# A decoder trunk on one core: the weight sums of a seven-product FFN step made in place, splits and sums in a fixed order, plain half steps between

## The chip, the cores and the metric

One core of a Trainium2 chip runs the whole kernel. The metric is device time in microseconds (us). TensorE (PE in the profile) multiplies, VectorE (DVE) and ScalarE (ACT) work element by element, SyncE (SP) issues the loads.

## What is computed

A two-layer decoder trunk in float32, 256 tokens of width 2048. Each layer has a mixer and a dense FFN, and it is the FFN that the change touches:

```python
D_MODEL = 2048; SEQ = 256; DEPTH = 2
D_FF = ((8 * D_MODEL + 3 * 256 - 1) // (3 * 256)) * 256     # 5632

def swiglu_ffn(h, w_gate, w_up, w_down):
    return (jax.nn.silu(h @ w_gate) * (h @ w_up)) @ w_down

for i in range(DEPTH):
    ...                                                     # mixer, residual
    f = swiglu_ffn(rms_norm(h, norm_gains[i, 2]), ffn_w_gate[i], ffn_w_up[i], ffn_w_down[i])
    h = h + rms_norm(f, norm_gains[i, 3])
```

## The kernel before

**Three matmuls for one.** Every float32 product is made of rounded parts. ACT copies a tile to a rounded high part (`whi`), DVE subtracts it from the tile to get the low part (`wlo`), and `mm3` (L212 to L214) issues three matmuls: high times high, high times low, low times high. So each weight that is loaded costs one ACT copy and one DVE subtraction: a split. There are four `whi` and four `wlo` buffers. They are handed out in the order of the splits, so a split takes the buffers of the one four before it and waits until TensorE has read those.

**The FFN.** Gate and up columns stand interleaved in blocks of 256. The 5632 hidden columns are made in five stages of 2, 2, 2, 2 and 3 chunks of 1024 gate-and-up columns; after each stage the down projection (`to_tokens`) uses what the stage made. The first stage is plain. In the other four, each chunk is 512 columns by plain products (`plain_step`) and 512 by a scheme of seven products in place of eight 2x2 block products (`seven_step`), four steps of each, over groups `g` of the 2048 rows. The seven-product step needs sums of weight blocks; DVE makes them in a room of its own (`ws`, tag `gb`, two buffers): three additions of 1024, 512 and 512 elements a partition. After the fourth step `seven_hidden` puts the seven products together, applies silu and multiplies; `hidden` does so for the plain half. `to_features` then turns the result on TensorE by four transposes (L418) and splits it again (L166, L167).

**PSUM.** Eight banks in two sets of four. `g4()` hands out the sets in turn. A stage takes one set for the seven products (`seven`) and the other for the plain half and the transposes (`other`). The next `g4()`, that of the down projection, is the set of `seven` again. In the order listings below, in one such stage, `seven` is bank2_78, bank3_79, bank6_82 and bank7_83; `other` is bank0_76, bank1_77 and, for transposes, bank4_80 and bank5_81.

**Order.** A scheduler sorts the instructions of each engine when the program is built; on the chip each engine then runs its list in that order, and an instruction that waits holds up all behind it on its engine. `issue_after` (here `behind`) puts one instruction behind another. The order of a chunk before:

```python
seven_step(col, g, seven)
if g == 3:
    behind_done()
    seven_hidden(seven, c * 4)
plain_step(col + 512, g, other[:2])
...
hidden(other[:2], c * 4 + 2, False)
```

Weights come through a ring of three tiles of 2048 elements a partition (`wst`). SP issues all loads in order.

Of the kernel before, what the change touches and what calls it, by code (L numbers as in the profile page):

```python
# [17 lines left out]
P = 128  # L18
# [30 lines left out]
def trunk(ctx, tc, x, mem, positions, norm_gains, w_mem_kv, w_down, a_w_in, a_b_s, a_w_out, w_kv_a, w_uk, w_uv,  # L49
# [118 lines left out]
        return ins.ins  # L168

    def wtile():  # L170
        return wpool.tile([P, 2048], F32, tag="wst", name="wst", bufs=3)

    def wsplit(src, n, gain=None):

# [101 lines left out]
                          in1=R.rearrange("p (o t) -> p o t", o=1).broadcast_to([P, n, S]), op=ALU.mult)  # L276

    def gain_bcast(i, j):
        g = tmp.tile([P, D], F32, tag="gb", name="gb", bufs=2)
        sp.dma_start(out=g, in_=norm_gains[i, j:j + 1, :].broadcast_to([P, D]))  # L280
        return g

# [119 lines left out]
    def ffn(i, xp, r, R, gcol, each, hp, need):  # L402
# [39 lines left out]
        def normalise(g):  # L442


            room = tmp.tile([P, D], F32, tag="gb", name="xr", bufs=2)
# [23 lines left out]
        def stage(col, g):  # L469

            st = wtile().rearrange("p (h k n) -> p h k n", h=2, k=2)
            rows = w_gate_up[i].rearrange("(h k p) n -> p h k n", h=2, p=P)
            for e in range(2):
                sp.dma_start(out=st[:, e], in_=rows[:, e, 2 * g:2 * g + 2, col:col + 512])
            return st

        def parts_of_sum(src, n=1024):
            hi = wpool.tile([P, 1024], F32R, tag="whi", name="whi", bufs=4)
            lo = wpool.tile([P, 1024], F32R, tag="wlo", name="wlo", bufs=4)
            hv, lv = hi[:, :n], lo[:, :n]  # L480
            if len(src.shape) == 4:
                hv, lv = [t.rearrange("p (h k n) -> p h k n", h=2, k=2) for t in (hv, lv)]
            elif len(src.shape) == 3:
                hv, lv = [t.rearrange("p (k n) -> p k n", k=2) for t in (hv, lv)]
            split(hv, lv, src)
            return hi, lo

        def seven_step(col, g, X):
            st = stage(col, g)
            room = tmp.tile([P, D], F32, tag="gb", name="ws", bufs=2)  # L490
            t13, t24 = room[:, :1024], room[:, 1024:]
            b11, b21, b22 = st[:, 0, :, :S], st[:, 1, :, :S], st[:, 1, :, S:]
            sums = room.rearrange("p (s k n) -> p s k n", s=4, k=2)
# [9 lines left out]
            wt = parts_of_sum(st[:, :, :, :S])  # L503
            dve.tensor_tensor(out=sums[:, 0:2], in0=st[:, :, :, S:], in1=st[:, 0].rearrange("p k (x n) -> p x k n", x=2),  # L504
                              op=ALU.add)
            products(wt, (xp, 0, 0, X[0][:, :S], True), (xp, 8, 0, X[0][:, S:], False))
            wt = parts_of_sum(t13)
            dve.tensor_tensor(out=sums[:, 2], in0=sums[:, 1], in1=b11, op=ALU.add)
            products(wt, (sz, 0, 0, X[1][:, S:], True), (sx, 0, 0, X[1][:, :S], False))
            dve.tensor_tensor(out=sums[:, 3], in0=sums[:, 2], in1=b21, op=ALU.add)  # L510
            wt = parts_of_sum(t24)
            products(wt, (sz, 0, 1, X[3][:, :S], True), (xp, 8, 1, X[2][:, :S], True))
            wt = parts_of_sum(b22, 512)
            products(wt, (sx, 0, 1, X[2][:, S:], False))

        def seven_hidden(X, f):

            m1, m2, m5, m6 = X[0][:, :S], X[0][:, S:], X[1][:, S:], X[3][:, :S]
            v = tmp.tile([P, 512], F32, tag="lat", name="v", bufs=2)
            act.copy(out=v[:, :S], in_=m1)  # L520
            dve.tensor_tensor(out=v[:, S:], in0=m6, in1=v[:, :S], op=ALU.add)
            u = tmp.tile([P, 512], F32, tag="lat", name="u", bufs=2)
            dve.tensor_tensor(out=u.rearrange("p (x n) -> p x n", x=2), in0=X[1].rearrange("p (x n) -> p x n", x=2),
                              in1=v[:, S:].rearrange("p (o n) -> p o n", o=1).broadcast_to([P, 2, S]), op=ALU.add)
            dve.tensor_tensor(out=m1, in0=m2, in1=v[:, :S], op=ALU.add)
            sg = tmp.tile([P, 512], F32, tag="sg", name="sg")
            act.activation(out=sg[:, :S], in_=m1, func=AF.Silu)
            dve.tensor_tensor(out=X[2], in0=X[2], in1=u, op=ALU.add)
            act.activation(out=sg[:, S:], in_=X[2][:, :S], func=AF.Silu)
            dve.tensor_tensor(out=m5, in0=m5, in1=u[:, :S], op=ALU.add)  # L530
            hv = tmp.tile([P, 512], F32, tag="hv", name="hv")
            for b, o in enumerate((X[2][:, S:], m5)):
# [5 lines left out]
        def plain_step(col, g, banks):  # L538
            st = stage(col, g)
            for e in range(2):  # L540
                wt = wsplit(st[:, e].rearrange("p k n -> p (k n)"), 1024)
# [17 lines left out]
        for pi, (c0, ncn) in enumerate(parts):  # L559
            if pi == 0:  # L560
# [30 lines left out]

            def gate(k):
# [31 lines left out]
    def start():  # L624
# [7 lines left out]
        m = []  # L632
        for b in range(2):
            yield
            t = tmp.tile([P, D], F32, tag="gb", name="memt", bufs=2)
            sp.dma_start(out=t, in_=mem[0, b * P:(b + 1) * P, :])
            m.append(t)
        yield
        yield from norm_scale(m, r_m, R_m)

# [77 lines left out]

    with tc.tile_pool(name="mixa", bufs=1) as ma:

        wT = tmp.tile([P, NH, P], F32, tag="gb", name="wT", bufs=2)
# [410 lines left out]
```

## Time and profile before

| | |
|---|---|
| median of 3 runs | 2118.49 us (2117.72 to 2119.36) |
| profiled execution: time, span in the trace | 2121.68 us, 2120.0 us |
| PE, DVE, ACT busy | 99%, 74%, 53% of the span |
| granted TensorE clock, mean | 0.998 |
| DMA engines busy | 56.4% by the kernel's queue |

The span runs from the first to the last instruction of the trace; the profiled execution takes 1.68 us more. TensorE's matmuls are pipelined and the ends that the profile gives are modelled, so that "busy" hides short pauses: the distance between the starts of two matmuls tells more than their length.

### The profile page before, as it was taken

What the parts mean: (1) busy time and instruction counts of PE and PEld (TensorE: products, weight loads), DVE (VectorE), ACT (ScalarE), POOL (GpSimd) and SP (SyncE); (2) the same over time, 40 slices, a digit from 0 to 9 for tenths busy, and PEclk for the clock granted to TensorE, in tenths of its full rate; (3) what the DMA queues carried; (4) which work ended last, traced back from release to release, by engine and by line L of the source; (5) the groups of instructions that cost most, each with busy time, mean ns of one, the idle gap of its engine ahead of it and who ended that gap; (6) DMA issues with size and microseconds to landing.
All of it is one profiled execution on the core that took longest, in us unless ns stands there. A gap on an engine that the chain in (4) does not pass through costs nothing.

```text
span 2120.0 us, 30041 instructions
## 1 busy us (share of the span) xinstructions
PE 2094.3 (99%) x11922; PEld 1835.1 (87%) x11922; DVE 1568.0 (74%) x2151; ACT 1119.4 (53%) x1478; POOL 4.1 (0%) x11
## 2 busy tenths in 40 slices
PE   8999999999999999999999999999999999999998
PEld 7889989788888888889889998978888888889987
DVE  6556755976868878689767775597686877868966
ACT  6544444655545545455545654565554554545543
POOL 0000000000000000000000000000000000000000
PEclk9999999999999999999999999999999999999999
DMA  9655365555565655655754534555556565565563
GB/s 359 250 181 174 92 221 185 178 181 177 195 202 179 201 179 186 209 178 199 242 176 136 181 122 140 183 174 189 177 190 200 178 218 179 189 207 168 199 222 130
DMA packets 153981, 398.96 MB, mean 188 GB/s; under 512 B 9456, under 2 KB 16880, under 8 KB 152816
## 3 DMA queue, kind: packets, MB, share of 16 engines
q1 hardware_dynamic: 153840, 397.05, 56.4%
q8 instruction: 93, 1.52, 0.3%
q14 instruction: 48, 0.39, 0.1%
HBM read 394.91 MB, written 2.10 MB: 187 GB/s over the span
## 4 chain that ended last, share of the span: by engine, by line
PE 91%; DVE 5%; DMA 2%; ACT 1%; issue 1%; SPq 0%; DVEq 0%; ACTq 0%
PE bank L214 29%; PE bank L213 29%; PE bank L212 29%; DMA wst<-in_w_gate_up 2%; PE bank L418 1%; DVE wlo L181 1%; DVE wlo L187 1%; DVE h L362 1%; PE bank L240 0%; PE bank L1016 0%; PE bank L1017 0%; DVE ws L504 0%; PE bank L707 0%; PE bank L1041 0%; DVE wlo L167 0%
## 5 line engine op out<-in xcount | busy, mean ns | idle before, releaser
L212 PE MATMUL bank<-whi,hl 128*128 128x512 f32 (+3 forms) x2880 | 1030.8, 359 | 0.9 <-ACT hl L166 0.7
L213 PE MATMUL bank<-wlo,hl 128*128 128x512 f32 (+3 forms) x2880 | 1026.6, 356 | 3.6 <-DVE wlo L181 1.9
L214 PE MATMUL bank<-whi,hl 128*128 128x512 f32 (+3 forms) x2880 | 1025.5, 356 | 0.0
L181 DVE TENSOR_TENSOR wlo<-wst,whi 128x1024 fp32r<-128x1024 f32 (+1 forms) x398 | 468.8, 1183 | 237.5 <-ACT whi L179 236.2
L213 PEld LDWEIGHTS bank<-wlo,hl 128*128 128x128 f32 x2880 | 542.3, 188 | 82.1 <-DVE wlo L181 4.1
L214 PEld LDWEIGHTS bank<-whi,hl 128*128 128x128 f32 x2880 | 542.3, 188 | 77.6 <-DVE hl L167 0.5
L212 PEld LDWEIGHTS bank<-whi,hl 128*128 128x128 f32 x2880 | 542.5, 188 | 76.2 <-ACT hl L166 1.9
L179 ACT CAST whi<-wst 128x1024 fp32r<-128x1024 f32 (+1 forms) x398 | 405.0, 1020 | 381.2 <-PE bank L214 346.3
L187 DVE SCALAR_TENSOR_TENSOR wlo<-wst,gains,whi 128x1024 fp32r<-128x1024 f32 (+3 forms) x216 | 255.7, 1193 | 131.0 <-ACT whi L185 128.1
L185 ACT ACTIVATE whi<-wst,gains 128x1024 fp32r<-128x1024 f32 (+3 forms) x216 | 232.2, 1080 | 216.7 <-PE bank L214 131.2
L166 ACT CAST whi<-ws 128x1024 fp32r<-128x1024 f32 x144 | 151.1, 1049 | 159.0 <-PE bank L214 81.0
L167 DVE TENSOR_TENSOR wlo<-ws,whi 128x1024 fp32r<-128x1024 f32 x144 | 175.6, 1220 | 57.0 <-ACT whi L166 56.8
L166 ACT CAST whi<-wst 128x1024 fp32r<-128x1024 f32 (+1 forms) x144 | 120.3, 835 | 108.1 <-PE bank L214 107.3
L167 DVE TENSOR_TENSOR wlo<-wst,whi 128x1024 fp32r<-128x1024 f32 (+1 forms) x144 | 137.0, 951 | 22.0 <-ACT whi L166 22.0
L212 PE MATMUL bank<-hl,whi 128*128 128x256 f32 x448 | 129.1, 288 | 7.0 <-ACT whi L185 7.0
L214 PE MATMUL bank<-hl,wlo 128*128 128x256 f32 x448 | 127.1, 285 | 1.0 <-DVE wlo L187 1.0
L213 PE MATMUL bank<-hl,whi 128*128 128x256 f32 x448 | 127.1, 284 | 0.0
L504 DVE TENSOR_TENSOR ws<-wst 128x1024 f32<-128x1024 f32 x72 | 88.0, 1223 | 26.1 <-DMA wst<-in_w_gate_up 25.7
L212 PEld LDWEIGHTS bank<-hl,whi 128*128 128x128 f32 x448 | 85.2, 190 | 10.2 <-ACT whi L185 7.0
L213 PEld LDWEIGHTS bank<-hl,whi 128*128 128x128 f32 x448 | 85.2, 190 | 2.8
L214 PEld LDWEIGHTS bank<-hl,wlo 128*128 128x128 f32 x448 | 84.8, 190 | 1.5 <-DVE wlo L187 1.4
L213 PE MATMUL bank<-wlo,sx 128*128 128x256 f32 x288 | 81.2, 282 | 0.0
(206 smaller groups left out, 1549.7 us busy)
## 6 DMA issues: line engine op xcount, KB each, us to landing
wst<-in_w_gate_up SPq DMA_DIRECT2D x288, 512.0 KB, 4.5
wst<-in_ffn_w_down SPq DMA_DIRECT2D x76, 1024.0 KB, 5.1
wst<-in_w_gate_up SPq DMA_DIRECT2D x32, 1024.0 KB, 4.9
wst<-in_a_w_in SPq DMA_DIRECT2D x24, 1024.0 KB, 5.1
wst<-in_w_mem_kv SPq DMA_DIRECT2D x15, 1024.0 KB, 6.5
wst<-in_ffn_w_down SPq DMA_DIRECT2D x12, 768.0 KB, 4.5
wst<-in_a_w_out SPq DMA_DIRECT2D x8, 1024.0 KB, 6.0
wst<-in_b_w_in SPq DMA_DIRECT2D x8, 1024.0 KB, 4.9
```

The lines of the kernel that those rows point to most:

```text
L166: ins = act.copy(out=hi, in_=src)
L167: dve.tensor_tensor(out=lo, in0=src, in1=hi.bitcast(F32), op=ALU.subtract)
L179: act.copy(out=hi[:, :n], in_=src)
L181: dve.tensor_tensor(out=lo[:, :n], in0=src, in1=hi[:, :n].bitcast(F32), op=ALU.subtract)
L185: act.activation(out=hi[:, :n], in_=src, func=AF.Copy, scale=g)
L187: dve.scalar_tensor_tensor(out=lo[:, :n], in0=src, scalar=g, in1=hi[:, :n].bitcast(F32), op0=ALU.mult, op1=ALU.subtract)
L212: pe.matmul(out=o, lhsT=a[0], rhs=b[0], start=start, stop=False, **kw)
L213: pe.matmul(out=o, lhsT=a[0], rhs=b[1], start=False, stop=False, **kw)
L214: line["pe"] = pe.matmul(out=o, lhsT=a[1], rhs=b[0], start=False, stop=stop, **kw).ins
L362: ins = dve.scalar_tensor_tensor(out=h[:, b, cs], in0=yv, scalar=rs[b], in1=h[:, b, cs], op0=ALU.mult, op1=ALU.add)
L418: pe.transpose(out=pt[:, q, b, :], in_=hv[:, b * S + q * P:b * S + (q + 1) * P], identity=ident)
L504: dve.tensor_tensor(out=sums[:, 0:2], in0=st[:, :, :, S:], in1=st[:, 0].rearrange("p k (x n) -> p x k n", x=2), op=ALU.add)
```

## The change

The ring of weight tiles has four tiles instead of three, and the rooms of tag `gb` one buffer instead of two (`mem` is read into the tile `h` for its norm). The seven-product step loads its four blocks by four transfers of 256 KB (runs of 1 KB) instead of two of 512 KB (runs of 2 KB), as up, up, gate, gate; first splits what it needs unsummed, then makes the sums in the tile itself, over blocks already split. All splits and sums of these stages are chained in one order. A plain step is cut in halves: one half ahead of the seven-product step, the other between its third product and the remaining four. With this the seven-product half of a chunk comes last, and `seven_hidden` after everything else; it now copies out of PSUM into `u` and `v` instead of summing in the banks. The counts and sizes of matmuls, splits and sums stay as they are.

```diff
-        return wpool.tile([P, 2048], F32, tag="wst", name="wst", bufs=3)
+        return wpool.tile([P, 2048], F32, tag="wst", name="wst", bufs=4)
...
+        def add(out, in0, in1):
+            with behind(last_on["dve"]):
+                after("dve", dve.tensor_tensor(out=out, in0=in0, in1=in1, op=ALU.add))
+
+        def own_split(src):
...
+            with behind(last_on["act"]):
+                after("act", act.copy(out=hi[:, :n], in_=src))
+            with behind(last_on["dve"]):
+                after("dve", dve.tensor_tensor(out=lo[:, :n], in0=src, in1=hi[:, :n].bitcast(F32), op=ALU.subtract))
...
+            for to, e, c in ((2, 0, gate), (3, 1, gate), (0, 1, up), (1, 0, up)):
+                sp.dma_start(out=q[:, to], in_=own[:, e, :, c])
...
+            ups, gates = st[:, :1024], st[:, 1024:]
+            wt = own_split(gates)
             products(wt, (xp, 0, 0, X[0][:, :S], True), (xp, 8, 0, X[0][:, S:], False))
+            wt = own_split(ups[:, :512])
+            products(wt, (sx, 0, 1, X[2][:, S:], True))
+            add(ups, ups, st[:, 512:1536])
+            add(q[:, 2], q[:, 0], q[:, 2])
+            add(q[:, 3], q[:, 2], q[:, 3])
+            between()
+            wt = own_split(ups)
+            products(wt, (sx, 0, 0, X[1][:, :S], True), (sz, 0, 0, X[1][:, S:], False))
+            wt = own_split(gates)
+            products(wt, (sz, 0, 1, X[3][:, :S], True), (xp, 8, 1, X[2][:, :S], False))
...
+            act.copy(out=v[:, :S], in_=X[0][:, :S])
+            dve.tensor_tensor(out=v[:, S:], in0=X[3][:, :S], in1=v[:, :S], op=ALU.add)
+            dve.tensor_tensor(out=v[:, :S], in0=X[0][:, S:], in1=v[:, :S], op=ALU.add)
...
-                        seven_step(col, g, seven)
-                        if g == 3:
-                            behind_done()
-                            seven_hidden(seven, c * 4)
-                        plain_step(col + 512, g, other[:2])
+                        plain = plain_steps(col, g, other[:2])
+                        next(plain)
+
+                        def between():
+                            next(plain)
+                            if g == 3:
+                                behind_done()
+                                hidden(other[:2], c * 4, False)
+
+                        seven_step(col + 512, g, seven, between)
                     behind_done()
-                    hidden(other[:2], c * 4 + 2, False)
+                    seven_hidden(seven, c * 4 + 2)
```

**The seam between a stage and its down projection, on DVE.** Such seams are eight: four stages in each layer. Before, from the first split of the down weights on (L181; `whi` names the split):

```order
L181 TENSOR_TENSOR wlo_5335<-wst_5332,whi_5334 128x1024 [waits DMAHW0_49,Activation_49]
L528 TENSOR_TENSOR bank6_82<-bank6_82,u_5274 128x512 [waits DVE_49,PE_49]
L530 TENSOR_TENSOR bank3_79<-bank3_79,u_5274 128x256
L181 TENSOR_TENSOR wlo_5357<-wst_5332,whi_5356 128x1024 [waits Activation_49]
L534 SCALAR_TENSOR_TENSOR hv_5282<-bank6_82,sg_5277 128x256 [waits Activation_49]
L534 SCALAR_TENSOR_TENSOR hv_5282<-bank3_79,sg_5277 128x256 [waits DVE_49]
L434 TENSOR_TENSOR hv_5327<-bank0_76,sg_5326 128x256 [waits Activation_49]
```

Now, from the same split on (L434 is `hidden`; L530, L531, L533, L535, L536 are the additions of `seven_hidden`):

```order
L181 TENSOR_TENSOR wlo_5341<-wst_5338,whi_5340 128x1024 [waits DMAHW1_49,Activation_49]
L434 TENSOR_TENSOR hv_5281<-bank0_76,sg_5280 128x256 [waits Activation_49]
L434 TENSOR_TENSOR hv_5281<-bank1_77,sg_5280 128x256 [waits Activation_49]
L181 TENSOR_TENSOR wlo_5363<-wst_5338,whi_5362 128x1024 [waits Activation_49]
L181 TENSOR_TENSOR wlo_5381<-wst_5378,whi_5380 128x1024 [waits DMAHW2_49,Activation_49]
L167 TENSOR_TENSOR hl01_73<-bank4_80,hl00_72 128x512 [waits Activation_49]
L530 TENSOR_TENSOR v_5324<-bank7_83,v_5324 128x256 [waits PE_49]
L181 TENSOR_TENSOR wlo_5397<-wst_5378,whi_5396 128x1024 [waits Activation_49]
L531 TENSOR_TENSOR v_5324<-bank2_78,v_5324 128x256 [waits DVE_49]
L533 TENSOR_TENSOR u_5325<-bank3_79,v_5324 128x512
L535 TENSOR_TENSOR v_5324<-bank3_79,u_5325 128x256 [waits DVE_49]
L536 TENSOR_TENSOR u_5325<-bank6_82,u_5325 128x512 [waits DVE_49,PE_49]
```

The plain half's `hv` moved ahead of the seven-product sums, and these now follow the third split of the down weights.

**The same seam on TensorE.** Before, the first matmuls of the down projection, which write bank2_78 first:

```order
L418 MATMUL bank4_80<-ident_84,hv_5282 128x128 x2
L212 MATMUL bank2_78<-whi_5334,hl00_72 128x512 [waits Activation_49]
L213 MATMUL bank2_78<-wlo_5335,hl00_72 128x512
L214 MATMUL bank2_78<-whi_5334,hl01_73 128x512
L212 MATMUL bank3_79<-whi_5334,hl00_72 128x512
```

Now, from the last matmul of the stage on:

```order
L214 MATMUL bank6_82<-whi_5308,hl11_75 128x256
L212 MATMUL bank7_83<-whi_5340,hl00_72 128x512 [waits DVE_49,Activation_49]
L213 MATMUL bank7_83<-wlo_5341,hl00_72 128x512
L214 MATMUL bank7_83<-whi_5340,hl01_73 128x512
L212 MATMUL bank7_83<-whi_5362,hl00_72 128x512 [waits Activation_49]
L213 MATMUL bank7_83<-wlo_5363,hl00_72 128x512
L214 MATMUL bank7_83<-whi_5362,hl01_73 128x512
L212 MATMUL bank7_83<-whi_5380,hl00_72 128x512 [waits Activation_49]
L212 MATMUL bank2_78<-whi_5340,hl00_72 128x512 [waits DVE_49]
```

The down projection now begins with seven matmuls into bank7_83, the first of which waits for DVE.

**From one chunk to the next inside a stage, on DVE.** There are ten such places. Before, from the first addition of `seven_hidden` (L525) on:

```order
L525 TENSOR_TENSOR bank2_78<-bank2_78,v_4839 128x256 [waits Activation_49]
L510 TENSOR_TENSOR ws_4903<-ws_4903,wst_4900 128x512 [waits DVE_49]
L181 TENSOR_TENSOR wlo_4857<-wst_4853,whi_4856 128x1024 [waits DMAHW6_49,Activation_49]
L521 TENSOR_TENSOR v_4839<-bank7_83,v_4839 128x256 [waits PE_49]
L181 TENSOR_TENSOR wlo_4879<-wst_4853,whi_4878 128x1024 [waits DMAHW7_49,Activation_49]
```

Now, from the next chunk's first gate split on (L480 are the sums in the tile; the last row is the split of that chunk's second plain half):

```order
L490 TENSOR_TENSOR wlo_4933<-wst_4927,whi_4932 128x1024 [waits DMAHW4_49,DMAHW3_49,Activation_49]
L490 TENSOR_TENSOR wlo_4949<-wst_4927,whi_4948 128x512 [waits DMAHW5_49,Activation_49]
L167 TENSOR_TENSOR hl01_73<-bank4_80,hl00_72 128x512 [waits Activation_49]
L530 TENSOR_TENSOR v_4888<-bank7_83,v_4888 128x256 [waits PE_49]
L480 TENSOR_TENSOR wst_4927<-wst_4927 128x1024 [waits DMAHW6_49,DVE_49]
L531 TENSOR_TENSOR v_4888<-bank2_78,v_4888 128x256 [waits DVE_49]
L533 TENSOR_TENSOR u_4889<-bank3_79,v_4888 128x512
L480 TENSOR_TENSOR wst_4927<-wst_4927 128x512 [waits DVE_49]
L535 TENSOR_TENSOR v_4888<-bank3_79,u_4889 128x256 [waits DVE_49]
L480 TENSOR_TENSOR wst_4927<-wst_4927 128x512 [waits DVE_49]
L536 TENSOR_TENSOR u_4889<-bank6_82,u_4889 128x512 [waits DVE_49,PE_49]
L490 TENSOR_TENSOR wlo_4962<-wst_4902,whi_4961 128x1024 [waits DMAHW2_49,Activation_49]
```

The additions of `seven_hidden` now stand between the next chunk's weight sums; before, they stood between the splits of the plain step of the same group. On TensorE, where before the whole next seven-product step followed, the list now goes on like this after the first products into bank2_78 (whi_4961 is the second plain half, whi_4977 the summed ups, whi_4948 the single up block):

```order
L214 MATMUL bank2_78<-whi_4932,hl11_75 128x256
L212 MATMUL bank0_76<-whi_4961,hl10_74 128x512 [waits Activation_49]
L212 MATMUL bank1_77<-whi_4961,hl10_74 128x512
L212 MATMUL bank3_79<-whi_4977,sx0_3360 128x256 [waits DVE_49,Activation_49]
L212 MATMUL bank6_82<-whi_4948,sx0_3360 128x256 [waits DVE_49]
L213 MATMUL bank6_82<-wlo_4949,sx0_3360 128x256
```

Three single matmuls were moved ahead of the six into bank6_82, which wait for DVE.

## Rows read from the trace of the kernel before

**Rows 1.** The page: busy us, share of the span, instructions.

```profile
PE 2094.3 (99%) x11922; PEld 1835.1 (87%) x11922; DVE 1568.0 (74%) x2151; ACT 1119.4 (53%) x1478; POOL 4.1 (0%) x11
```

**Rows 2.** Waits of TensorE's weight loads, 512 to 1100 us: total, times, longest.

```profile
PEld bank L213 <- DVE wlo L181: 2.4, 4, 1.6
PEld bank L418 <- DVE hv L534: 1.5, 3, 0.6
```

**Rows 3.** The same waits, 1528 to 2110 us.

```profile
PEld bank L418 <- DVE hv L534: 1.4, 3, 0.6
PEld bank L213 <- DVE wlo L181: 0.8, 2, 0.4
```

**Rows 4.** Timeline, PE at 776 us: start, length, line; twelve and six matmuls.

```profile
775.85 0.40 PE L214 MATMUL bank<-whi,hl 128*128 128x512 f32 x1
...
776.78 0.28 PE L212 MATMUL bank<-whi,hl 128*128 128x256 f32 x1
...
777.38 0.28 PE L214 MATMUL bank<-whi,hl 128*128 128x256 f32 x1
```

**Rows 5.** Timeline, PE at 866 us: the four transposes.

```profile
866.01 0.60 PE L418 MATMUL bank<-ident,hv 128*128 128x128 f32 x4
866.36 0.48 PE L212 MATMUL bank<-whi,hl 128*128 128x512 f32 x1
```

**Rows 6.** Timeline, 759 to 761 us: one split, from TensorE to ACT to DVE.

```profile
759.98 0.40 PE L212 MATMUL bank<-whi,hl 128*128 128x512 f32 x1
...
760.18 1.05 ACT L179 CAST whi<-wst 128x1024 fp32r<-128x1024 f32 x1 [1.75 <-PE bank L214]
...
761.26 1.22 DVE L181 TENSOR_TENSOR wlo<-wst,whi 128x1024 fp32r<-128x1024 f32 x1 [1.57 <-ACT whi L179]
```

**Rows 7.** Timeline, DVE at 858 us: work that follows without a pause.

```profile
858.40 1.21 DVE L181 TENSOR_TENSOR wlo<-wst,whi 128x1024 fp32r<-128x1024 f32 x1
859.53 0.69 DVE L528 TENSOR_TENSOR bank<-bank,u 128x512 f32<-128x512 f32 x1
860.13 0.42 DVE L530 TENSOR_TENSOR bank<-bank,u 128x256 f32<-128x256 f32 x1
860.47 1.21 DVE L181 TENSOR_TENSOR wlo<-wst,whi 128x1024 fp32r<-128x1024 f32 x1
```

**Rows 8.** Timeline, ACT at 857 to 864 us: two copies, silu, the transposes' copy.

```profile
856.73 2.01 ACT L179 CAST whi<-wst 128x1024 fp32r<-128x1024 f32 x2 [0.35 <-PE bank L214]
...
862.27 0.38 ACT L433 ACTIVATE sg<-bank 128x256 f32<-128x256 f32 x1 [0.71 <-PE bank L214]
...
864.30 0.59 ACT L166 CAST hl<-bank 128x512 fp32r<-128x512 f32 x1
```

**Rows 9.** Timeline, 667 to 672 us: a late load and TensorE's wait.

```profile
667.33 1.23 DVE L504 TENSOR_TENSOR ws<-wst 128x1024 f32<-128x1024 f32 x1 [2.55 <-DMA wst<-in_w_gate_up]
...
671.67 0.50 PE L213 MATMUL bank<-wlo,hl 128*128 128x512 f32 x1 [1.27 <-DVE wlo L181]
```

**Rows 10.** Waits of the whole span: total, times, longest.

```profile
DVE ws L504 <- DMA wst<-in_w_gate_up: 25.7, 35, 2.6
```

**Rows 11.** Windows: length, busy (instructions) of PE, PEld, DVE, ACT, POOL, clock, DMA share, GB/s.

```profile
670.00:690.00 20.00, 18.73 (x110) 15.92 (x109) 18.56 (x25) 10.84 (x16) 0.00 (x0) 1.00 0.65 211
1095.00:1107.00 12.00, 11.08 (x88) 10.71 (x86) 11.24 (x29) 8.44 (x16) 0.00 (x0) 1.00 0.57 182
1107.00:1112.00 5.00, 4.11 (x12) 2.54 (x12) 3.65 (x17) 1.25 (x5) 0.00 (x0) 0.66 0.49 197
```

**Rows 12.** Timeline, 36 to 47 us: the norm of `mem`, the load of `x`.

```profile
36.22 0.19 ACT L233 ACTIVATION_READ_ACCUMULATOR junk<-memt 128x1 f32 x1
...
46.60 0.47 SPq L669 DMA_DIRECT2D h<-in_x  x1
```

**Rows 13.** DMA issues, 277 to 366 us: KB each, us to landing (L312, 1 KB runs).

```profile
wst<-in_a_w_out SPq DMA_DIRECT2D x4, 512.0 KB, 3.9
```

**Rows 14.** DMA issues of the page, the steps' loads (2 KB runs).

```profile
wst<-in_w_gate_up SPq DMA_DIRECT2D x288, 512.0 KB, 4.5
```

More of the change, by code (lines that the diff above doesn't have):

```diff
@@ L278, in gain_bcast @@
     def gain_bcast(i, j):
-        g = tmp.tile([P, D], F32, tag="gb", name="gb", bufs=2)
+        g = tmp.tile([P, D], F32, tag="gb", name="gb", bufs=1)
         sp.dma_start(out=g, in_=norm_gains[i, j:j + 1, :].broadcast_to([P, D]))
@@ L442, in normalise @@
         def normalise(g):
-            room = tmp.tile([P, D], F32, tag="gb", name="xr", bufs=2)
+            room = tmp.tile([P, D], F32, tag="gb", name="xr", bufs=1)
             xr = room[:, :1024].rearrange("p (h k t) -> p h k t", h=2, k=2)
@@ L467, in normalise @@
             yield
[L469 to L477, printed above, removed]
+        rows = w_gate_up[i].rearrange("(h k p) n -> p h k n", h=2, p=P)
+        last_on = {"dve": None, "act": None}
@@ L478, in parts_of_sum, with after @@
+        def after(engine, ins):
+            last_on[engine] = ins.ins
+            return ins
+        def add(out, in0, in1):
+            with behind(last_on["dve"]):
+                after("dve", dve.tensor_tensor(out=out, in0=in0, in1=in1, op=ALU.add))
+        def own_split(src):
             hi = wpool.tile([P, 1024], F32R, tag="whi", name="whi", bufs=4)
             lo = wpool.tile([P, 1024], F32R, tag="wlo", name="wlo", bufs=4)
[L480 to L484, printed above, removed]
@@ L485, in parts_of_sum @@
-            split(hv, lv, src)
-            return hi, lo
[L488 to L493, printed above, removed]
+            n = src.shape[-1]
+            with behind(last_on["act"]):
+                after("act", act.copy(out=hi[:, :n], in_=src))
@@ new lines, in own_split, with seven_step @@
+            with behind(last_on["dve"]):
+                after("dve", dve.tensor_tensor(out=lo[:, :n], in0=src, in1=hi[:, :n].bitcast(F32), op=ALU.subtract))
+            return hi, lo
+        def seven_step(col, g, X, between):
+            st = wtile()
+            q = st.rearrange("p (q k n) -> p q k n", q=4, k=2)
+            own = rows[:, :, 2 * g:2 * g + 2, :]
+            gate, up = slice(col, col + S), slice(col + S, col + 2 * S)
+            for to, e, c in ((2, 0, gate), (3, 1, gate), (0, 1, up), (1, 0, up)):
+                sp.dma_start(out=q[:, to], in_=own[:, e, :, c])
@@ L509, in seven_step @@
[L509 to L514, printed above, removed]
+            wt = own_split(ups[:, :512])
+            products(wt, (sx, 0, 1, X[2][:, S:], True))
+            add(ups, ups, st[:, 512:1536])
@@ L516, in seven_hidden @@
+            add(q[:, 2], q[:, 0], q[:, 2])
[5 more added lines that the diff above has]
+            products(wt, (sz, 0, 1, X[3][:, :S], True), (xp, 8, 1, X[2][:, :S], False))
         def seven_hidden(X, f):
-            m1, m2, m5, m6 = X[0][:, :S], X[0][:, S:], X[1][:, S:], X[3][:, :S]
             v = tmp.tile([P, 512], F32, tag="lat", name="v", bufs=2)
-            act.copy(out=v[:, :S], in_=m1)
@@ L521, in seven_hidden @@
-            dve.tensor_tensor(out=v[:, S:], in0=m6, in1=v[:, :S], op=ALU.add)
             u = tmp.tile([P, 512], F32, tag="lat", name="u", bufs=2)
+            sg = tmp.tile([P, 512], F32, tag="sg", name="sg")
+            act.copy(out=v[:, :S], in_=X[0][:, :S])
+            dve.tensor_tensor(out=v[:, S:], in0=X[3][:, :S], in1=v[:, :S], op=ALU.add)
+            dve.tensor_tensor(out=v[:, :S], in0=X[0][:, S:], in1=v[:, :S], op=ALU.add)
+            act.activation(out=sg[:, :S], in_=v[:, :S], func=AF.Silu)
@@ L523, in seven_hidden @@
             dve.tensor_tensor(out=u.rearrange("p (x n) -> p x n", x=2), in0=X[1].rearrange("p (x n) -> p x n", x=2),
                               in1=v[:, S:].rearrange("p (o n) -> p o n", o=1).broadcast_to([P, 2, S]), op=ALU.add)
[L525 to L528, printed above, removed]
@@ L529, in seven_hidden @@
-            act.activation(out=sg[:, S:], in_=X[2][:, :S], func=AF.Silu)
-            dve.tensor_tensor(out=m5, in0=m5, in1=u[:, :S], op=ALU.add)
+            dve.tensor_tensor(out=v[:, S:], in0=X[1][:, S:], in1=u[:, :S], op=ALU.add)
+            dve.tensor_tensor(out=u, in0=X[2], in1=u, op=ALU.add)
+            act.activation(out=sg[:, S:], in_=u[:, :S], func=AF.Silu)
             hv = tmp.tile([P, 512], F32, tag="hv", name="hv")
-            for b, o in enumerate((X[2][:, S:], m5)):
+            for b, o in enumerate((u[:, S:], v[:, S:])):
@@ L536, in seven_hidden, with plain_steps @@
             bg.append(behind_group[-1])
-        def plain_step(col, g, banks):
-            st = stage(col, g)
+        def plain_steps(col, g, banks):
+            st = wtile().rearrange("p (h k n) -> p h k n", h=2, k=2)
             for e in range(2):
-                wt = wsplit(st[:, e].rearrange("p k n -> p (k n)"), 1024)
+                sp.dma_start(out=st[:, e], in_=rows[:, e, 2 * g:2 * g + 2, col:col + 512])
+            for e in range(2):
+                wt = own_split(st[:, e].rearrange("p k n -> p (k n)"))
                 for j in range(2):
@@ L547, in plain_step @@
                 tick()
+                yield
         early = list(range(4)) + list(range(8, 12)) + list(range(4, 8)) + list(range(12, 16))
@@ L577, in ffn @@
             else:
+                last_on.update(dve=None, act=None)
                 seven, other = g4(), g4()
@@ L634, in start @@
             yield
-            t = tmp.tile([P, D], F32, tag="gb", name="memt", bufs=2)
-            sp.dma_start(out=t, in_=mem[0, b * P:(b + 1) * P, :])
-            m.append(t)
+            sp.dma_start(out=h[:, b, :], in_=mem[0, b * P:(b + 1) * P, :])
+            m.append(h[:, b, :])
         yield
@@ L719, in trunk @@
     with tc.tile_pool(name="mixa", bufs=1) as ma:
-        wT = tmp.tile([P, NH, P], F32, tag="gb", name="wT", bufs=2)
+        wT = tmp.tile([P, NH, P], F32, tag="gb", name="wT", bufs=1)
         sp.dma_start(out=wT, in_=w_sT.rearrange("s (g t) -> s g t", t=P))
```

5 lines of the change are left out of this document (removed).

## The prediction

> **What bounds the kernel now.** I read the page's busy times first: TensorE is busy 99% of the span, VectorE (DVE) 74%, ScalarE 53% [rows 1]. A modelled 99% can hide pauses, so I read next what TensorE's weight loads wait for in the two stretches that hold all the seven-product stages. In both together they wait 3.2 us for low parts of splits (2.4 and 0.8) and 2.9 us for the products that are to be transposed (1.5 and 1.4): 6.1 us in over 1100 [rows 2, 3]. So TensorE runs there at its own pace. The reader is to see that pace in the starts: from 775.85 to 776.78 are four steps, 0.2325 us for a matmul of 512 columns, and from 776.78 to 777.38 five, 0.12 for one of 256 [rows 4]; four transposes take 0.35 [rows 5]. The change leaves matmuls as they are. It can save at most those 6.1 us, and it can cost whatever TensorE must newly wait for. The question is where DVE is late.
>
> **The change part by part.** Counts and sizes of splits and sums stay. A fourth weight tile lets loads start a tile earlier. A late load is seen at 667.33: DVE waited 2.55 us for it, and 4 us later TensorE waited 1.27 [rows 9]; DVE waits 35 times for such loads, 25.7 us in all [rows 10]. I take it that the waits for low parts go: **minus 3.2 us** (bounds 0 and 6.1).
>
> Three edits I cost at nothing. Runs of 1 KB: 512 KB in such runs land after 3.9 us, in 2 KB runs after 4.5 [rows 13, 14]; six issues a pair of steps instead of four cost SP 2 x 0.47 us [rows 12] of 10.6, where it otherwise waits for tiles. Without that cover a late load costs the 1.27 us seen above. `mem` in `h`: its norm ends at 36.4 and `x` is loaded into `h` at 46.6 [rows 12]. One `gb` buffer: the sums, its heavy user, are gone from it; if a gain vector's load had to wait there, SP would hold the weights' loads behind it, and the price is again a late load's 1.27.
>
> The two moved seams cost. Take a chunk's last pair of steps from its first matmul, t = 0, and call the parts A1 (plain half), G (gates), B (one up block), A2 (second plain half), U and S (summed ups, summed gates). From [rows 4, 5]: A1 12 x 0.2325 = 2.79, G 12 x 0.12 = 1.44, B 0.72, A2 2.79, U 1.44, four transposes 0.35, S 1.44. They end at 2.79, 4.23, 4.95, 7.74, 9.18, 9.53 and 10.97. For the chain between engines [rows 6]: ScalarE starts a copy 0.20 after TensorE turned to the next group (760.18 - 759.98), the copy takes 1.05, DVE follows 0.03 later (761.26 - 761.23). DVE work without a pause goes at distances of 1.13 (1024 elements), 0.60 (512) and 0.34 (256); one alone lasts 1.22, 0.69, 0.42 [rows 7]. A silu takes 0.38, the copy of a transposed bank 0.59 [rows 8]. From DVE to TensorE I take 0.05.
>
> *Stage to down projection, 8 times.* The second silu of the plain half waits for A2: 7.94 to 8.32. The second down split (call it K1) takes A2's buffers: copy 8.32 to 9.37, on DVE from 9.40, which is free again at 10.53. The third (K2) takes U's buffers: copy 9.38 to 10.43, on DVE 10.53 to 11.66. Then stands, by the listing, the low part of the transposed plain half (its copy 10.43 to 11.02): 11.66 to 12.26. Only then comes L530, which reads bank7_83: it ends at 12.68. That bank was complete at about 10.25, and S ends at 10.97; the down projection's first matmul, into bank7_83, starts at 12.73. TensorE stands still for **1.76 us**. After its seven matmuls there (to 14.36) the next bank is free: L531 ends at 12.60 + 1.13 + 0.42 = 14.15. Before, the same matmuls wrote a bank that had been read long before: `seven_hidden` lay under a plain step of 5.6 us. Bounds: nothing, if L530's turn came when bank7_83 is complete (10.25 + 0.20 + 0.42 + 0.05 = 10.92); with full lengths instead of distances (9.40 + 1.22 + 1.22 + 0.69 + 0.42 + 0.05) 13.0, so 2.03.
>
> *Chunk to chunk, 10 times (one in each stage of two, two in each of three).* Next chunk's A1 runs on TensorE from 10.97 to 13.76 and covers much. DVE: the gate split from 9.40, B's from 10.53, the transposed half 11.13, L530 11.73, first sum 12.07, L531 13.20, L533 13.54, second sum 14.14, L535 14.74, third sum 15.08, L536 15.68 to 16.37, A2's low part 16.28 to 17.50. TensorE finds bank2_78 free (13.62) at 13.76, ends G at 15.20, does the three single matmuls (0.585, to 15.79) and waits for bank6_82 until 16.42: 0.63. B ends at 17.14, two more of 256 at 17.38, A2's low part is there at 17.55: 0.17. Together **0.80 us**. Bounds: nothing; with full lengths throughout L536 ends at 17.24 and A2's low part at 18.46, and the waits are 1.50 and 0.26, so 1.76. Elsewhere in a chunk DVE is in time: G from 9.40, B 10.53, the three sums 11.13, A2's low part 13.46 to 14.68, wanted at 10.62 + 4.95 = 15.57. And what is late at a seam is caught up: DVE's work for a chunk is about 39 us (four times 8.6 for splits and sums, 4.8 for the rest) of TensorE's 43.
>
> Sum: 8 x 1.76 + 10 x 0.80 - 3.2 = 14.1 + 8.0 - 3.2 = **+18.9 us**. The durations are those of the profiled execution (2121.68 us: span 2120.0 and 1.68 around it), which would become 2140.6. It stands 3.2 above the median of 2118.49, so I predict 2118.49 + 18.9 = **2137.4 us**.
>
> *Does the clock fall at the new pauses?* After the pause of 1.27 us at 670 the granted clock is 1.00 in the window to 690. It falls once in this stretch of the program: from 1095 to 1107 TensorE is busy 11.08 of 12 us at 1.00, and in the 5 us after that, with 12 matmuls, the mean is 0.66 [rows 11]: some 3.4 us at the lower level (1.2 instead of 2.4 GHz), which lose 1.7. I price no fall, since the new pauses are like the one at 670. The Trainium skill (TensorE: Matmul & The Clock Gate, section A second HAM failure mode: psum-queue depth-cycling) says that short idle spells between groups of matmuls, with banks in rotation, can make the clock swing and cost throughput. The trace shows nothing of it at 670.
>
> **The rivals.** *DVE is not late at the stage ends (no change).* For it: in [rows 7] DVE works through such a chain at the short distances, and the scheduler that built the lists chose bank7_83 as the first to come free. Against it: K2's copy cannot start before U has ended, and K2 stands ahead of L530. Time: with pauses of 0 to 0.4 us at the 18 places, 2118.49 - 3.2 = 2115.3 to 2122.5.
>
> *The loads were the matter (faster).* If L530 got its turn by 10.45, 1.8 us earlier than I work out, there is no seam, and if the fourth tile takes all the waits of [rows 2, 3], the time is 2118.49 - 6.1 = 2112.4. It decides from there: every 0.3 us of mean pause over the 18 places takes 5.4 of the 6.1 us back. For it speaks the late load at 667; against it that so few of the 35 waits of DVE reach TensorE.
>
> *The clock falls at each stage end (slower still).* 8 x 1.7 = 13.6 us more: 2151.0. Against it stands the window at 670. The skill's page named above is the rule behind it.
>
> **How the numbers follow.** A measurement of this kernel tells about 0.2% (4.2 us) from no change: 2114.3 to 2122.7. Forecast, pauses at both kinds of seam: 0.75, from 2123 (seams at 1.0, inner places at 0.3, 6.1 us saved: +4.9) to 2152.3 (upper bounds, nothing saved: +33.8). No lateness: 0.12. Loads: 0.08, of which all is faster. Clock: 0.05, slower. So faster 0.08, same 0.12, slower 0.80. The range starts at 2121, which leaves out the faster case and most of the unchanged one, and ends at 2152, which takes in the clock case and the upper bounds.
>
> **What would show it.** In the profile after: waits of TensorE's matmuls on L530's tile `v` at eight places, 1.8 us each, and on `u` (L536) at ten, 0.6 us; DVE's waits for the loads of gate and up nearly gone; splits' low parts no longer waited for elsewhere; TensorE's distances unchanged; the clock at 1.00 in the stages. I am wrong if L530 starts by 10.5 us after the chunk's last pair began, or if DVE falls behind inside a chunk, where I found 0.9 us to spare at A2.

## The result, and the profile after

The changed kernel takes **2135.84 us** (median of 4 runs, 2134.78 to 2137.30), the kernel before in the same comparison 2118.75 (2117.72 to 2119.36): ratio 1.0082, 95% interval 1.0064 to 1.0099. It is slower by 17.1 us; 18.9 were forecast. Its profiled execution takes 2137.3 us, with a span of 2135.6, which is 15.6 more than before.

The page's busy times of the changed kernel, which answer to [rows 1], hardly tell it: TensorE's share has gone from 99% to 98%.

```profile
PE 2095.8 (98%) x11922; PEld 1836.9 (86%) x11922; DVE 1590.4 (74%) x2151; ACT 1127.7 (53%) x1478; POOL 3.7 (0%) x11
```

The waits do. First those of the matmuls in the changed kernel, 512 to 1118 us (releaser, total, times, longest); the second half of the program has the same two rows, 6.3 and 1.6:

```profile
PE bank L212 <- DVE v L530: 6.3, 4, 1.6
PE bank L212 <- DVE u L536: 1.6, 5, 0.3
```

Then those of the weight loads, same kernel and stretch, beside [rows 2]:

```profile
PEld bank L212 <- ACT whi L179: 7.0, 4, 1.8
PEld bank L212 <- DVE u L536: 3.2, 5, 0.6
```

Four waits for L530 and five for L536 in each half are the eight stage ends and the ten inner places. No low part and no `hv` of the stages is waited for any more. The two views name different releasers for the same four pauses: the bank (L530) or the weights' high part (ACT, L179). The timeline settles it. The end of the first stage in the changed kernel (start, length, engine, line; idle time and releaser in brackets):

```profile
594.99 2.20 ACT L179 CAST whi<-wst 128x1024 fp32r<-128x1024 f32 x2
596.07 2.38 DVE L181 TENSOR_TENSOR wlo<-wst,whi 128x1024 fp32r<-128x1024 f32 x2 [0.51 <-ACT whi L179]
597.09 0.58 ACT L166 CAST hl<-bank 128x512 fp32r<-128x512 f32 x1
597.68 0.28 PE L214 MATMUL bank<-whi,hl 128*128 128x256 f32 x1
598.36 0.68 DVE L167 TENSOR_TENSOR hl<-bank,hl 128x512 fp32r<-128x512 f32 x1
598.96 0.41 DVE L530 TENSOR_TENSOR v<-bank,v 128x256 f32<-128x256 f32 x1
599.49 0.19 PEld L212 LDWEIGHTS bank<-whi,hl 128*128 128x128 f32 x1 [1.74 <-ACT whi L179]
599.52 0.47 PE L212 MATMUL bank<-whi,hl 128*128 128x512 f32 x1 [1.56 <-DVE v L530]
```

The copies K1 and K2, made after the one that this matmul needs, end at 597.19, and TensorE's next weight load comes at 599.49: ScalarE can't be the releaser. DVE has no gap from 596.07 on: K1 and K2, the transposed half, L530 to 599.37, and TensorE goes on 0.15 later. The stage's last matmul starts at 597.68 and would be followed after 0.12; the pause is 1.84 - 0.12 = 1.72. At all eight ends the distance is 1.84 to 1.90, the mean pause 1.73.

An inner place of the changed kernel, from the transposed half on:

```profile
553.94 0.68 DVE L167 TENSOR_TENSOR hl<-bank,hl 128x512 fp32r<-128x512 f32 x1
554.54 0.41 DVE L530 TENSOR_TENSOR v<-bank,v 128x256 f32<-128x256 f32 x1
554.87 1.22 DVE L480 TENSOR_TENSOR wst<-wst 128x1024 f32<-128x1024 f32 x1
...
557.87 0.68 DVE L480 TENSOR_TENSOR wst<-wst 128x512 f32<-128x512 f32 x1
558.47 0.68 DVE L536 TENSOR_TENSOR u<-bank,u 128x512 f32<-128x512 f32 x1
558.62 0.28 PE L212 MATMUL bank<-whi,sx 128*128 128x256 f32 x1
559.07 1.22 DVE L490 TENSOR_TENSOR wlo<-wst,whi 128x1024 fp32r<-128x1024 f32 x1
559.20 0.39 PE L212 MATMUL bank<-whi,sx 128*128 128x256 f32 x1 [0.31 <-DVE u L536]
```

DVE is busy from the transposed half to L536's end at 559.15; TensorE waits from 558.74 to 559.20, 0.46. (The 0.31 in brackets is counted from a modelled end; the starts tell more.) Over the ten places the distance is 0.588 to 0.615, the mean pause 0.48.

The clock in the changed kernel, in the stretch of the pause and in the one behind it (length, busy time and instructions of PE, PEld, DVE, ACT, POOL, clock, DMA share, GB/s), as in [rows 11]: it stays at 1.00.

```profile
597.00:600.00 3.00, 1.44 (x11) 1.21 (x10) 3.00 (x5) 1.72 (x3) 0.00 (x0) 1.00 0.88 284
600.00:606.00 6.00, 6.00 (x29) 4.90 (x29) 4.03 (x8) 2.37 (x4) 0.00 (x0) 1.00 0.80 281
```

### The profile page after: what moved, and what is told of

It is laid out like the page before. It is cut to its first block, busy times and chain, and to the rows that moved or that the text cites. A ratio compares the mean times of both kernels' runs of the same rounds, so it can differ in the third digit from the quotient of the medians.

```text
span 2135.6 us, 30440 instructions
## 1 busy us (share of the span) xinstructions
PE 2095.8 (98%) x11922; PEld 1836.9 (86%) x11922; DVE 1590.4 (74%) x2151; ACT 1127.7 (53%) x1478; POOL 3.7 (0%) x11
## 4 chain that ended last, share of the span: by engine, by line
PE 89%; DVE 7%; ACT 2%; issue 2%; DMA 0%; SPq 0%; DVEq 0%; ACTq 0%
PE bank L214 28%; PE bank L213 28%; PE bank L212 28%; ACT whi L488 1%; DVE wst L480 1%; DVE hl L167 1%; DVE wlo L181 1%; DVE wlo L490 1%; DVE wlo L187 1%; PE bank L418 1%; DVE h L362 0%; ACT whi L179 0%; PE bank L240 0%; PE bank L1032 0%; PE bank L1033 0%
## 5 line engine op out<-in xcount | busy, mean ns | idle before, releaser
L488 ACT CAST whi<-wst 128x1024 fp32r<-128x1024 f32 (+1 forms) x432 | 418.8, 979 | 340.0 <-PE bank L214 212.7
L490 DVE TENSOR_TENSOR wlo<-wst,whi 128x1024 fp32r<-128x1024 f32 (+1 forms) x432 | 475.8, 1133 | 94.1 <-ACT whi L488 90.6
L181 DVE TENSOR_TENSOR wlo<-wst,whi 128x1024 fp32r<-128x1024 f32 (+1 forms) x254 | 295.1, 1165 | 233.6 <-ACT whi L179 233.1
L179 ACT CAST whi<-wst 128x1024 fp32r<-128x1024 f32 (+1 forms) x254 | 254.4, 1002 | 293.2 <-PE bank L214 281.4
L480 DVE TENSOR_TENSOR wst<-wst 128x512 f32<-128x512 f32 (+1 forms) x216 | 187.5, 868 | 6.2
L212 PE MATMUL bank<-whi,sx 128*128 128x256 f32 x288 | 81.9, 284 | 3.2 <-DVE u L536 3.2
L214 PE MATMUL bank<-whi,sx 128*128 128x256 f32 x288 | 81.4, 282 | 0.0
```

What stands on the lines that cost most here:

```text
L179: act.copy(out=hi[:, :n], in_=src)
L181: dve.tensor_tensor(out=lo[:, :n], in0=src, in1=hi[:, :n].bitcast(F32), op=ALU.subtract)
L212: pe.matmul(out=o, lhsT=a[0], rhs=b[0], start=start, stop=False, **kw)
L214: line["pe"] = pe.matmul(out=o, lhsT=a[1], rhs=b[0], start=False, stop=stop, **kw).ins
L480: after("dve", dve.tensor_tensor(out=out, in0=in0, in1=in1, op=ALU.add))
L488: after("act", act.copy(out=hi[:, :n], in_=src))
```

## The experiments

All start from the changed kernel. Each ratio is to the kernel before, measured with it. The median of the kernel before was 2118.75 us beside the changed kernel and 2119.20 to 2119.75 beside the runs below, so differences of medians that were not measured together are uncertain by about 1 us.

| run | median, us | ratio to before, 95% interval |
|---|---|---|
| `first_sum_early` | 2122.04 | 1.0014 (1.0005 to 1.0023) |
| `other_banks` | 2122.48 | 1.0013 (1.0004 to 1.0022) |
| `sums_after_half` | 2132.13 | 1.0057 (1.0044 to 1.0069) |
| `three_tiles` | 2170.37 | 1.0235 (1.0221 to 1.0249) |
| `both` | 2120.63 | 1.0004 (0.9995 to 1.0013) |
| `other_both` | 2120.22 | 1.0003 (0.9994 to 1.0012) |
| `late_by_one` | 2155.20 | 1.0168 (1.0155 to 1.0182) |
| `free_order` | 2136.25 | 1.0079 (1.0065 to 1.0093) |
| `other_first` | 2121.83 | 1.0008 (0.9998 to 1.0017) |
| `early_first` | 2120.73 | 1.0003 (0.9994 to 1.0012) |

**first_sum_early**: is it L530's place in DVE's list?

```diff
-            dve.tensor_tensor(out=v[:, S:], in0=X[3][:, :S], in1=v[:, :S], op=ALU.add)
+            first = dve.tensor_tensor(out=v[:, S:], in0=X[3][:, :S], in1=v[:, :S], op=ALU.add)
...
+            return first.ins
...
-                    seven_hidden(seven, c * 4 + 2)
+                    first = seven_hidden(seven, c * 4 + 2)
+                line.update(after=first, act=line["act"], first=2, left=1)
```

> The first addition of seven_hidden (L530) goes ahead of the third split of the down weights and of the transposed half on DVE, nothing else is meant to change. Theory (the place in DVE's list decides): L530 ends about when the stage's last matmul starts, the eight pauses of 1.73 us at the down projection shrink to 0.05, so 2135.84 - 8 x 1.68 = 2122.4 us. Rival 1 (TensorE waits there for the copies of the down weights, which its weight loads name as releaser with 7.0 us in four waits of one half of the program): pauses stay, 2136. Rival 2 (the pause only moves on, to bank2_78 or to the low part of the third split, 0.3 to 1.0 us late): 2125 to 2131.

13.8 us of the 17.1 went. The stage end in this run:

```profile
595.23 1.22 DVE L181 TENSOR_TENSOR wlo<-wst,whi 128x1024 fp32r<-128x1024 f32 x1 [0.51 <-ACT whi L179]
596.45 0.42 DVE L530 TENSOR_TENSOR v<-bank,v 128x256 f32<-128x256 f32 x1
596.85 0.28 PE L214 MATMUL bank<-whi,hl 128*128 128x256 f32 x1
597.02 0.47 PE L212 MATMUL bank<-whi,hl 128*128 128x512 f32 x1
```

L530 ends at 596.87, when the stage's last matmul has just begun, and the down projection follows after 0.17. L531 and the 512-element addition behind it moved ahead of K2's low part too; this, put off to 598.40, holds nobody up. So DVE's order alone made the pause, and it didn't move on; both rivals fall.

**other_banks**: the same wait taken away from the other side, with DVE as late as ever.

```diff
                     seven_hidden(seven, c * 4 + 2)
+                turns["g"] += 1
+                short["banks"] = seven[2:]
```

> The down projection starts in the banks of the plain half and of its transposes, which are read about 3 us before, instead of in those of the seven products; the transposes of the seven products then go to two banks of these. DVE's list keeps L530 where it was at the stage's end. Theory (the pause is the wait for a bank that L530 reads late): eight pauses of 1.73 us go, 2122.0 us, though DVE is as late as before. Rival (DVE is late with the low parts of the down weights themselves, or the copies are): pauses stay, 2136; or the banks of the transposes come free too late (their low part ends 1.7 us after the stage's last matmul group began): 0.5 to 1.0 us stay, 2126 to 2130.

13.4 us less. In this run's stage end the first matmul of the down projection starts at 596.15, 0.12 after the last of the stage; L530 comes 1.2 us later and nobody waits for it:

```profile
596.03 0.28 PE L214 MATMUL bank<-whi,hl 128*128 128x256 f32 x1
596.15 0.39 PE L212 MATMUL bank<-whi,hl 128*128 128x512 f32 x1
...
597.31 0.41 DVE L530 TENSOR_TENSOR v<-bank,v 128x256 f32<-128x256 f32 x1
```

DVE's lateness costs only where the next bank depends on it. The low parts of the down weights and the copies are in time.

**sums_after_half**: the inner places.

```diff
+            between()
             add(ups, ups, st[:, 512:1536])
             add(q[:, 2], q[:, 0], q[:, 2])
             add(q[:, 3], q[:, 2], q[:, 3])
-            between()
```

> The three weight sums in the tile are issued behind the second plain half's split instead of ahead of it, so at the inner places the sums of seven_hidden no longer stand between them on DVE. Theory (L536 is late because the weight sums stand ahead of it): the ten pauses of 0.47 to 0.50 us go, the eight at the stage ends stay: 2135.84 - 4.8 = 2131.0 us. Rival (ten pauses are set by L536's own chain of four additions, or the summed ups come late instead): 2135 to 2138.

3.7 us less, where 4.8 were expected, and not from the ten places alone. No wait for L536 is left. But the stage ends, which were to stay, shrank as well. The matmuls' waits in this run, 512 to 1118 us and 1528 to 2130 us, where the changed kernel has 6.3 in each:

```profile
PE bank L212 <- DVE v L530: 4.4, 4, 1.4
PE bank L212 <- DVE v L530: 5.5, 4, 1.4
```

By the starts, seven of the eight pauses are 1.48 to 1.58 us and one is 0.32, 2.6 us less in all. So 7.4 us of pauses went for a gain of 3.7. What took the rest back shows in the waits of the weight loads in this run, 1528 to 2130 us, as rows that the changed kernel hadn't: transposes wait for the plain half's products, and matmuls for low parts, 0.2 us at a time.

```profile
PEld bank L418 <- DVE hv L434: 1.7, 10, 0.2
PEld bank L213 <- DVE wlo L490: 1.0, 5, 0.2
```

**three_tiles**: what the fourth tile is worth.

```diff
-        return wpool.tile([P, 2048], F32, tag="wst", name="wst", bufs=4)
+        return wpool.tile([P, 2048], F32, tag="wst", name="wst", bufs=3)
```

> The changed kernel with the ring of three weight tiles instead of four, all else as changed. Theory of the prediction (the fourth tile is what takes the waits of 3.2 us for late loads, the lateness of DVE sets the new pauses): 2135.84 + 2 to 4 = 2138 to 2140 us, the pauses at the eighteen places as before. Rival 1 (the sums in place, which free the tile earlier or later, made the loads punctual and the tile does nothing): 2135.8. Rival 2 (in-place sums hold a tile to the step's end, so that three are too few and every pair of steps waits): over 2150.

34.5 us slower than the changed kernel. My theory falls, and rival 2 has the size. ScalarE's waits over this run's whole span have the weights' loads as a large row, where the changed kernel has 7.2 us in 9 waits:

```profile
ACT whi L488 <- DMA wst<-in_w_gate_up: 108.1, 84, 3.8
```

SP's load of a seven-product step (L500) waits 54 times for a split to free its tile, 8 us on average:

```profile
SPq L500 <- DVE wlo L490: 429.1, 54, 12.5
```

In the changed kernel it waits as often, but 1.7 us:

```profile
SPq L500 <- DVE wlo L490: 93.4, 56, 2.8
```

Which split it is, the timelines tell. In this run the load starts within 0.4 us after the low part of A2, the second half of a plain step, in 64 of 72 steps; in the changed kernel it is after that of S, the last split of a seven-product step, in 56 of 72. The tiles alternate between plain and seven-product steps, so with three of them a seven-product step's load takes the tile of the plain step one pair before, and with four that of a seven-product step two pairs before. One such load with three tiles (DVE's row is A2, ScalarE's is G of the next pair):

```profile
672.98 1.22 DVE L490 TENSOR_TENSOR wlo<-wst,whi 128x1024 fp32r<-128x1024 f32 x1
674.23 1.91 SPq L500 DMA_DIRECT2D wst<-in_w_gate_up  x4
677.79 1.05 ACT L488 CAST whi<-wst 128x1024 fp32r<-128x1024 f32 x1 [1.95 <-DMA wst<-in_w_gate_up]
```

From the first of the four issues, a gate block's, to the copy of G are 3.6 us in the median, about what such a load takes to land (3.9 in this run); with four tiles they are 11.9. All 84 waits are for blocks of seven-product steps. The plain steps' loads, which take the tiles that held the sums, start 9.0 us ahead of their first copy, and none is waited for. So what makes three tiles too few is the plain step's second half, which the change put between the products of a seven-product step, and not, as rival 2 had it, the sums in the tile: in the kernel before, too, the last split of a seven-product step (L513) read the loaded tile. The 34.5 us also hold longer pauses at the stage ends (2.05 to 3.67 us) and five falls of the clock behind them. What a fourth tile would bring to the kernel before was not tried: its two rooms for sums leave no space for one. Nor were the sums in place tried without the halved plain step.

**late_by_one**: a dose.

```diff
+            dve.tensor_copy(out=u, in_=X[3])
             dve.tensor_tensor(out=v[:, S:], in0=X[3][:, :S], in1=v[:, :S], op=ALU.add)
```

> A dose: in the changed kernel DVE copies bank7_83 (512 elements) to u once more, right ahead of L530; u is written again by L533, so results are the same. Theory (L530's end sets the pause at the stage ends, L536's at the inner places): with 0.60 us for the copy the pauses grow from 1.73 to 2.3 and from 0.48 to 1.1, 18 x 0.6 = 10.8 more, 2146.6 us. Rival 1 (something other than DVE's chain releases TensorE): 2136. Rival 2 (the clock falls at pauses of over 2 us, as the run with three tiles shows at five of eight stage ends, eight matmuls of 0.427 instead of 0.233 us): up to 8 x 1.5 on top, 2150 to 2159.

19.4 us more than the changed kernel, 8.6 more than the dose. The stage end in this run (L530 is the copy here, L531 the sum):

```profile
597.30 0.28 PE L214 MATMUL bank<-whi,hl 128*128 128x256 f32 x1
598.58 0.68 DVE L530 COPY u<-bank 128x512 f32<-128x512 f32 x1
599.18 0.41 DVE L531 TENSOR_TENSOR v<-bank,v 128x256 f32<-128x256 f32 x1
599.74 0.47 PE L212 MATMUL bank<-whi,hl 128*128 128x512 f32 x1 [2.17 <-DVE v L531]
...
602.61 0.63 PE L213 MATMUL bank<-wlo,hl 128*128 128x512 f32 x1
603.04 0.63 PE L214 MATMUL bank<-whi,hl 128*128 128x512 f32 x1
```

The copy takes 0.60 of DVE's list, and the distance at the stage ends grows from 1.84 to 2.44, by just that; at the inner places from 0.60 to 1.11, by 0.51. That is 8 x 0.60 + 10 x 0.51 = 9.9. The rest is the clock. From 600.51 on, matmuls of 512 columns follow at 0.427 us in place of 0.233. This run's windows behind the pause of the first stage, and behind that of the fourth:

```profile
600.00:604.00 4.00, 4.00 (x12) 3.13 (x12) 3.58 (x7) 0.83 (x2) 0.00 (x0) 0.57 0.80 275
604.00:608.00 4.00, 4.00 (x21) 3.29 (x20) 0.90 (x1) 1.66 (x3) 0.00 (x0) 1.00 0.30 119
...
1053.00:1058.00 5.00, 5.00 (x24) 4.11 (x25) 3.77 (x7) 1.17 (x3) 0.00 (x0) 1.00 0.89 307
```

At five of the eight stage ends it falls, to 0.57 in the first, for about eight matmuls; at three it doesn't, after pauses of the same length. Some 40 such matmuls lose 0.19 each, 7.7 us, or 1.55 a fall. Theory and rival 2 hold together: 9.9 and 7.7 make 17.6, and the span is 16.6 longer than the changed kernel's, whose trace has a fall of about 1.1 us at the end of the first layer that this one lacks (see the last section).

**free_order**: the fixed order by itself. In `add` and `own_split`, three times:

```diff
-            with behind(last_on["dve"]):
+            with behind(None):
```

> The changed kernel without its chain of splits and sums: the scheduler may order them as it finds best; at the stage ends and the inner places DVE's list reads as with the chain. Theory (the places cost, not the chain): 2135 to 2137. Rival (the fixed order holds DVE or ScalarE up elsewhere): under 2132.

2136.25, and the waits for L530 and L536 as in the changed kernel. The chain costs nothing. For ScalarE this is no trial of it, since its list comes out the same without the chain; DVE's differs in 130 of 2151 places.

**both** (`first_sum_early` with `sums_after_half`) and **other_both** (`other_banks` with `sums_after_half`):

> first_sum_early and sums_after_half together: no pauses left at the eight stage ends nor at the ten inner places. Theory (pauses at two kinds of place, independent of each other): 2122.0 - 3.7 (what sums_after_half gave alone) = 2118.3 us, so about the kernel before, and no better, since what the change saved is small. Rival (the splits of the second plain half, brought forward, push the sums of seven_hidden back at the stage ends): pauses of 0.3 us and more come back, 2120 us or more. Rival 2 (the loads were the matter, so that without pauses the full 6.1 us show): 2112 to 2114 us.

> other_banks and sums_after_half together. Theory: 2122.5 - 3.7 = 2118.8 us, and since the bank no longer depends on DVE's place at the stage ends, at most that. Rival (transposes wait more for the plain half's products, as in sums_after_half alone, and this now counts at the stage ends): 2120 us or more.

2120.63 and 2120.22: the kernel before, within the uncertainty, and 1.4 to 2.3 us above the sums of the single effects. About as much as that `sums_after_half` had gained at the stage ends, where these two have nothing more to gain. No pause for L530 or L536 is left in `other_both`, and in `both` a single one for L530, 0.33 us at 1035; the loads' rival with its 2112 to 2114 falls. In `other_both` TensorE's weight loads wait, from 512 to 1118 us, as in `sums_after_half`:

```profile
PEld bank L418 <- DVE hv L434: 1.5, 9, 0.2
...
PEld bank L213 <- DVE wlo L490: 1.0, 5, 0.2
```

**other_first** and **early_first**: the moved sums in a chunk's first step alone, to be rid of these rows.

```diff
+            if g == 0:
+                between()
             add(ups, ups, st[:, 512:1536])
...
-            between()
+            if g:
+                between()
```

> other_banks, with the weight sums behind the second plain half's split in a chunk's first step of four alone, where the sums of seven_hidden stand in DVE's list; in the other three steps they stay ahead of it. Theory (the rest that other_both leaves is small waits of 0.1 to 0.2 us of the transposes for the plain half's products and of TensorE for low parts, brought by the moved sums at the last step of a chunk, 1.5 and 1.0 us in each half of the program): 2120.2 - 3 = 2117 us, 2 to 3 us under the kernel before, which is what the saved waits for low parts are worth. Rival (these small waits lie beside others and give nothing): 2120 us.

> first_sum_early with the weight sums moved in a chunk's first step alone. Theory: 2120.6 - 3 = 2117.6 us. Rival (nothing): 2120.6 us.

2121.83 and 2120.73: nothing gained. The transposes no longer wait for L434, but in `other_first` two rows of 1.8 us stand in the same stretch where `other_both` has 1.5 and 1.0:

```profile
PEld bank L212 <- ACT whi L488: 1.8, 5, 0.4
PEld bank L213 <- DVE wlo L490: 1.8, 5, 0.4
```

A change of order from a chunk's first step to its second leaves the low parts and copies there late. None of these versions is faster than the kernel before.

## Why the prediction was right

**Stage to down projection: right in cause and size.** 1.76 was worked out, 1.73 measured, 8 x 1.73 = 13.8 us. The places of K1, K2, the transposed half and L530 came at the distances of [rows 7], 0.14 earlier against the stage's end than worked out (L530 ends 1.57 after it, worked out 1.71), and TensorE took 0.15 to go on where 0.05 had been assumed. That these two errors nearly cancel is luck; both are small against 1.73. Two edits that take the wait away, one on each side of it, give back 13.8 and 13.4, and a dose of 0.60 comes out as 0.60.

**Chunk to chunk: right in cause, too large.** 0.63 and 0.17 were worked out. The bank's wait is 0.48, since DVE is some 0.15 earlier there too; A2's low part, ready at 560.29, is read at 560.34, some 0.1 late. By the starts of the matmuls, ten places cost nearer 6 than 8.0 us. No run shows that size by itself: `sums_after_half`, which ends the pauses, shortens the stage ends too and brings small waits, and on top of `first_sum_early` and `other_banks` it gave 1.4 and 2.3.

**The late loads: the term came out, the reason was half wrong.** The waits of [rows 2, 3] are gone. The span's 15.6 are 13.8 + 5.8 less some 4; the medians' 17.1 leave 2.5. 3.2 had been taken. This is a remainder, no measurement of its own: in the trace before, the matmuls of the seven-product stages that start over 0.25 us late sum to 2.4 us, 1.4 of it the one at 670; its execution stands 3.2 us above the median, and how many of the waits of [rows 2, 3] were its own stays open. Half wrong was that a fourth tile "lets loads start a tile earlier" and so takes waits away. The new order of the steps needs it first: without it 34.5 us are lost. Nor do the runs show a gain to be had behind the pauses. With them gone, the two stretches from the first seven-product stage to the end of the layer's FFN take 1185.4 us (`both`) and 1184.8 us (`other_both`) together in the traces, and 1184.9 before.

**The edits costed at nothing: right.** The two kinds of step loads in the changed kernel (KB each, us to landing) compare with [rows 13, 14]; DVE, which waited 25.7 us for them [rows 10], has 3.1 left, and ScalarE, whose copy now comes first, waits 7.2. The room of `gb` and `mem` in `h` were not tried apart; up to the first seven-product stage the changed kernel's trace is 0.8 us shorter than that of before. The loads after the change:

```profile
wst<-in_w_gate_up SPq DMA_DIRECT2D x144, 512.0 KB, 4.5
wst<-in_w_gate_up SPq DMA_DIRECT2D x288, 256.0 KB, 4.0
```

**The clock: no fall, as forecast, but by a small margin.** I argued from one pause of 1.27 us. At 1.73 it holds at all eight ends; at 2.32 it falls at five of eight. That 1.73 lies on the safe side nothing in the trace before could tell, so this part was in some measure luck. The rival's price of 1.7 us a fall was about right: 1.55 measured in `late_by_one`. Its chance of 0.05 rested on a single pause. The Trainium skill (TensorE: Matmul & The Clock Gate, section A second HAM failure mode: psum-queue depth-cycling) says that short idle spells between groups of matmuls can make the clock swing. The trace of `late_by_one` agrees with that at five of its eight stage ends; the trace of the change shows no swing at any of its eight.

## What to carry to other kernels

When a reduction is moved to the end of a stage, look at who needs the bank that it reads: put it first in the vector engine's list, or let the next stage start in a bank that is already read. Each is worth the whole pause, and the engine's total load says nothing about it. When a step is cut in two and another step's products are put between the halves, its tile is held until the second half is split: count then which tile of the ring each load must wait for, and how long before its first use that tile comes free.

## What the runs showed of the hardware

The granted clock doesn't follow from a pause's length alone. After the same 2.44 us between starts it fell at five stage ends and stayed at three. At the end of the first layer TensorE waits twice in each of these kernels, with 1.2 and 1.0 us between starts. There it fell to 0.66 in the kernel before [rows 11]; in `first_sum_early` it stayed:

```profile
1106.00:1111.00 5.00, 4.41 (x21) 3.02 (x22) 4.63 (x19) 1.59 (x6) 0.00 (x0) 1.00 0.93 383
```

Of the twelve traces seven have this fall (before, after, `sums_after_half`, `three_tiles`, `free_order`, `other_first`, `early_first`). From the layer's last FFN matmul to the next layer's first seven-product stage they take 412.4 to 412.9 us, the other five 411.4 to 411.7: the fall costs about 1.1 us here. So the profiled executions of two kernels that differ elsewhere can stand some 1 us apart for this alone, as those of `first_sum_early` and `other_banks` do from that of the changed kernel. What decides it, and how often it falls in the executions that were not profiled, no run here shows.
